# Gated products of a feed-forward transposed as float32r, by way of a transfer

## The chip, the cores and the metric

The kernel runs on one core of a Trainium2 chip. The metric is the device time of one execution in microseconds: the median of the runs. The core's engines are TensorE (PE: products and transposes; PEld: the loading of its weights), VectorE (DVE), ScalarE (ACT), GpSimd (POOL) and SyncE (SP), which issues most transfers (DMA) here. Each engine takes its instructions in order and waits at semaphores for the others.

## The reference, cut to what matters

Two layers, each with two feed-forwards around a token mixer, on 256 tokens of width 1024. So there are four feed-forwards, with an inner width of 2816:

```python
def swiglu(x, w_gate, w_up, w_down):
    return (jax.nn.silu(x @ w_gate) * (x @ w_up)) @ w_down
...
    f = swiglu(rms_norm(h, ffn1_pre_g[layer]), ffn1_w_gate[layer], ffn1_w_up[layer], ffn1_w_down[layer])
    h = h + 0.5 * rms_norm(f, ffn1_post_g[layer])
```

The change touches the product silu(x @ w_gate) * (x @ w_up), which must be turned round (channels to partitions) before it is multiplied with w_down. All inputs and outputs are float32.

## The kernel before, in words

**Precision.** TensorE multiplies in float32r, a narrower form of float32. To keep float32's precision, every operand is split in two float32r parts, hi (rounded) and lo (the rest), and every product is three: hi by hi, lo by hi, hi by lo (`mm3`, lines 179 to 183, giving L181, L182 and L183). A weight block is loaded into a float32 tile raw (five buffers), split by ScalarE (whi, L171) and VectorE (wlo, L175) into one of nine pairs of buffers, and then used by both token halves.

**Tiles and slots.** The 256 tokens are two halves, t = 0 and 1, of 128. A feed-forward (`ffn_items`, line 482) is a list of items, each a block of weights: for each of five chunks of 512 inner columns four items for the gate and four for the up product (two rows of 128 of the 1024 inputs in each), then four items for the last chunk of 256 columns, gate and up side by side in one bank (`pair_items`), then 22 items for the down product (`row_items`, one row block of w_down each). A slot (`slot`, line 365) is one item for one half: six float32r products of 512 columns. `run` (line 374) gives out the slots: half 0 goes some items ahead of half 1, soon four, and then they take turns.

**A chunk.** When the gate's sum of a half is done, ScalarE makes sil, the silu of it (L496). When the up product's sum is done, VectorE makes prod from sum and sil (L507, `post_up`). TensorE then transposes prod in blocks of 128x128 against a float32 identity into a bank tr (L515, `hidden_T`), and ScalarE and VectorE make from tr the parts hhi (L519) and hlo (L520), the operands of the down product. In `mm<-whi,xhi` the second name is the operand that sits in the array; in `tr<-ident,prod` prod sits in it and the identity streams through.

**Order.** TensorE's order is written out by the program (`tc.manual_schedule`); on the other engines a scheduler orders instructions. `defer(n, fn)` (line 81) puts a piece of work into a list, and `tick` (line 84), called at the end of each slot, runs it when its count has gone below zero: n = 2 runs two slots after the slot in which it was put there. In the kernel before, `post_up` collects both halves' prod in `made`, and when half 1 is done it defers the transposes of both by HT = 2 slots: eight transposes in a row, four in the last chunk. prod has two buffers in its pool.

**Queues.** SP issues the weight loads, the gain vectors and the small gate weights, each in its place in SP's order; a load waits on SP until the subtraction (L175) that last read its raw buffer is done. All of these go through one queue, whose transfers are spread over 16 DMA engines. `prepare_next` (line 346) decides by a pace that the program keeps by itself when the next item's load and split are put in the order.

Of the kernel before, what the change touches and what calls it, by code (L numbers as in the profile page):

```python
# [9 lines left out]
F32 = mybir.dt.float32  # L10
F32R = mybir.dt.float32r
# [5 lines left out]
P = 128  # L17
# [10 lines left out]
EPS = 1e-6  # L28
RAW = 5
WB = 9  # L30
HT = 2
LAG = 7
MID = 4
NEG = -1e30
# [10 lines left out]
def trunk_kernel(ctx: ExitStack, tc: tile.TileContext, A: dict, out: bass.AP):  # L45
    nc = tc.nc
# [3 lines left out]
    cpool = ctx.enter_context(tc.tile_pool(name="const", bufs=1))  # L50
    wpool = ctx.enter_context(tc.tile_pool(name="w", bufs=1))
    hpool = ctx.enter_context(tc.tile_pool(name="h", bufs=1))
    spool = ctx.enter_context(tc.tile_pool(name="small", bufs=4))
# [4 lines left out]
    def nm(s):  # L58
        uid[0] += 1
        return f"{s}_{uid[0]}"  # L60
# [7 lines left out]
    def trbank():  # L68
        return psum.tile([P, 512], F32, tag="tr", name=nm("tr"), bufs=2)
# [11 lines left out]
    def defer(n, fn):  # L81
        pend.append([n, fn])
# [26 lines left out]

        q.dma_start(h[t][:, a * P:b * P], A["x"][0, t * P:(t + 1) * P, a * P:b * P])  # L110

    grow0 = cpool.tile([16, P], F32, name="grow0")
    nc.scalar.dma_start(grow0, A["ffn1_pre_g"].rearrange("l (k p) -> (l k) p", p=P))
    ident = cpool.tile([P, P], F32, name="ident")
    make_identity(nc, ident)
    mhalf = cpool.tile([P, 1], F32, name="mhalf")
    nc.gpsimd.memset(mhalf, -0.5)
    warm = cpool.tile([P, 1], F32, name="warm")
# [208 lines left out]
    def gain_bcast(src):  # L327
        gb = hpool.tile([P, D], F32, tag="gb", name=nm("gb"), bufs=1)
        nc.sync.dma_start(gb, src.partition_broadcast(P))
        return gb  # L330
# [58 lines left out]
    def proj_items(w, c0, nn, get_x, post, nk=8):  # L389

        kper = min(1024 // nn, 4)
        acc = {}

        for k0 in range(0, nk, kper):
            kn = min(kper, nk - k0)

            def fetch(k0=k0, kn=kn, pieces=1):
                return load_raw(w[k0 * P:(k0 + kn) * P, c0:c0 + nn].rearrange("(k p) n -> p k n", p=P), P, kn * nn, pieces)

            def prep(fetch=fetch, kn=kn):  # L400
                return split(fetch(), P, kn * nn)

            def work(t, u, k0=k0, kn=kn, i=len(items)):
                if i < OPEN:
                    if k0 + kn == nk:
                        post(t, first_acc[t][:, :nn])
                    return
                if k0 == 0:
                    acc[t] = mmbank()
                ps = acc[t][:, :nn]  # L410
                for j in range(kn):
                    k = k0 + j
                    mm3(ps, *get_x(t, k), u.hi[:, j * nn:(j + 1) * nn], u.lo[:, j * nn:(j + 1) * nn], k == 0, k == nk - 1)
                if k0 + kn == nk:
                    post(t, acc[t][:, :nn])
            if len(items) < OPEN:
                first_loads.append(fetch)
            items.append((prep, work))

    def pair_items(wa, wb, c0, nn, get_x, post):  # L420

        acc = {}

        for k0 in range(0, 8, 2):
            def prep(k0=k0):
                raw = new_raw()
                v = raw.rearrange("p (k s n) -> p k s n", k=2, s=2)
                for s, w in enumerate((wa, wb)):
                    nc.sync.dma_start(v[:, :, s, :], w[k0 * P:(k0 + 2) * P, c0:c0 + nn].rearrange("(k p) n -> p k n", p=P))
                return split(raw, P, 1024)  # L430

            def work(t, u, k0=k0):
                if k0 == 0:
                    acc[t] = mmbank()
                for j in range(2):
                    k = k0 + j
                    mm3(acc[t], *get_x(t, k), u.hi[:, j * 512:(j + 1) * 512], u.lo[:, j * 512:(j + 1) * 512], k == 0, k == 7)
                if k0 == 6:
                    post(t, acc[t][:, :nn], acc[t][:, nn:2 * nn])
            items.append((prep, work))  # L440

    def row_items(w, widths, get_x, post, rows=2, rows0=2, late=False):

        acc = {}
        kept = [[], []]
        nk = len(widths)
        r0 = 0
        for k, kp in enumerate(widths):  # L450
            def prep(kp=kp, r0=r0, k=k):
                return split(load_raw(w[r0:r0 + kp, :], kp, D), kp, D, pin=late and k > 3)

            def work(t, u, k=k):
                if k == 0:
                    acc[t] = [mmbank(), mmbank()]
                m = rows if t == 1 else rows0
                if k >= nk - m:
                    kept[t].append((k, u))
                    if k < nk - 1:  # L460
                        return
                    todo = [(kk, uu, n) for n in range(2) for (kk, uu) in kept[t]]
                else:
                    todo = [(k, u, n) for n in range(2)]
                for (kk, uu, n) in todo:
                    mm3(acc[t][n], *get_x(t, kk), uu.hi[:, n * 512:(n + 1) * 512], uu.lo[:, n * 512:(n + 1) * 512],
                        kk == 0, kk == nk - 1)
                if k == nk - 1:
                    post(t, acc[t])
            items.append((prep, work))  # L470
            r0 += kp

    def ahead(i, fn):

        prep, work = items[i]

        def both():
            fn()
            return prep()
        items[i] = (both, work)  # L480

    def ffn_items(pool_of, wg, wu, wd, post_g, next_dests, last=False, normed=False):
        hid = {}
        sil = {}
        box = {}

        def hid_tiles(t):
            if t not in hid:
                hid[t] = (pool_of().tile([P, 22, P], F32R, tag=f"hhi{t}", name=nm("hhi"), bufs=1),
                          pool_of().tile([P, 22, P], F32R, tag=f"hlo{t}", name=nm("hlo"), bufs=1))  # L490
            return hid[t]

        def post_gate(c0, nn):
            def f(t, ps):
                s = pool_of().tile([P, 512], F32, tag="sil", name=nm("sil"), bufs=2)
                nc.scalar.activation(s[:, :nn], ps, AF.Silu, scale=rs[t][:, 0:1])  # L496
                sil[t] = s
            return f

        def post_up(c0, nn):  # L500
            made = []

            def f(t, ps):
                hh, hl = hid_tiles(t)
                s = sil[t][:, :nn]
                pr = pool_of().tile([P, 512], F32, tag="prod", name=nm("prod"), bufs=2)
                nc.vector.scalar_tensor_tensor(pr[:, :nn], ps, rs[t][:, 0:1], s, ALU.mult, ALU.mult)  # L507
                made.append((pr, hh, hl))
                if t == 1:
                    defer(HT, lambda: [hidden_T(*m) for m in made])  # L510

            def hidden_T(pr, hh, hl):
                tp = trbank()
                for j in range(nn // P):
                    nc.tensor.transpose(tp[:, j * P:(j + 1) * P], pr[:, j * P:(j + 1) * P], ident)  # L515
                k0 = c0 // P
                hv = hh[:, k0:k0 + nn // P, :].rearrange("p a b -> p (a b)")
                lv = hl[:, k0:k0 + nn // P, :].rearrange("p a b -> p (a b)")
                nc.scalar.activation(hv, tp[:, :nn], AF.Copy)  # L519
                nc.vector.tensor_tensor(lv, tp[:, :nn], hv.bitcast(F32), ALU.subtract)  # L520
            return f

        i0 = len(items)
        for i in range(5):
            proj_items(wg, i * 512, 512, main_x, post_gate(i * 512, 512))
            proj_items(wu, i * 512, 512, main_x, post_up(i * 512, 512))

        last_up = post_up(2560, 256)

        def post_both(t, pg, pu):  # L530
            post_gate(2560, 256)(t, pg)
            last_up(t, pu)

        pair_items(wg, wu, 2560, 256, main_x, post_both)

        def load_gb():
            box["gb"] = gain_bcast(post_g)

        ahead(i0 + 24, load_gb)

        def post_down(t, accs):
            enter(t, next_dests(t), accs, box["gb"], True, last, normed)

        row_items(wd, [P] * 22, lambda t, k: (hid[t][0][:, k, :], hid[t][1][:, k, :]), post_down, 4 if last else 2)
        return i0
# [803 lines left out]
```

## Time and profile before

| | |
|---|---|
| median of 3 runs | 990.96 us (990.84 to 990.96) |
| the profiled execution, first to last instruction (span) | 989.2 us |
| TensorE busy | 981.0 us, 99% of the span |
| weight loads of TensorE busy | 817.2 us, 83% |
| VectorE busy | 616.4 us, 62% |
| ScalarE busy | 528.0 us, 53% |
| queue 1 (weight loads) | 177.42 MB, 58.1% of 16 DMA engines' span |
| L515, the transposes of prod | 176 |
| L507, prod | 48 (40 of 128x512, 8 of 128x256) |

A row of the groups reads: line, engine, operation, written tile <- read tiles, shape, count, then the time in which the group was busy (us), the mean of one (ns), and the engine's idle time ahead of them. A row of the timeline reads: start (us), duration, engine, line, operation, tiles, shape, count, and in brackets the idle time before it and what ended it. TensorE's instructions overlap: the next starts while the last columns of the one before are still on their way, so the distance of starts, not the duration, tells what one costs. SPq is SP's issue of a transfer, not its flight. A row of the windows gives, for a stretch of time, its length, then busy time and instructions of each engine, then TensorE's granted clock, the DMA engines' share and GB/s.

### The profile page before, as it was taken

The numbers are of one execution on the slowest core, as the hardware profiler recorded it, in microseconds if no ns is written. First come the engines' busy times: TensorE is split into PE (matmuls) and PEld (weight loads), VectorE is DVE, ScalarE is ACT, GpSimd is POOL, SyncE is SP. The second block draws the span as 40 slices with busy tenths as digits, with TensorE's granted clock in tenths as the row PEclk, the third lists the DMA queues.
The fourth block names the chain that finished last, engine by engine and source line by source line (L and its number), as shares of the span: only waits on it lengthen the run. The fifth ranks groups of instructions, "written<-read, shape, count | busy, mean of one in ns | idle before, by whom it ended". The sixth has DMA issues, their size and how long they took to land.

```text
span 989.2 us, 12913 instructions
## 1 busy us (share of the span) xinstructions
PE 981.0 (99%) x4775; PEld 817.2 (83%) x4775; DVE 616.4 (62%) x790; ACT 528.0 (53%) x753; POOL 47.1 (5%) x92
## 2 busy tenths in 40 slices
PE   9999999999999999999999999999999999999997
PEld 6888888898978888888898888888888788888886
DVE  6756554678997555554686655554488876555542
ACT  7545443568986544443564444444366755444431
POOL 2400000100003000000100000000020000000000
PEclk9999999999999999999999999999999999999999
DMA  8967556465346766656567666655552467665531
GB/s 293 312 187 206 191 190 191 151 200 161 119 126 196 215 188 186 191 182 192 133 203 239 178 185 190 192 173 190 190 172 65 126 197 212 190 191 191 180 120 42
DMA packets 92645, 178.89 MB, mean 181 GB/s; under 512 B 11966, under 2 KB 30822, under 8 KB 92582
## 3 DMA queue, kind: packets, MB, share of 16 engines
q1 hardware_dynamic: 91142, 177.42, 58.1%
q8 instruction: 37, 0.61, 0.3%
q10 hardware_dynamic: 608, 0.53, 0.2%
q0 software_dynamic: 832, 0.12, 0.1%
q14 instruction: 26, 0.21, 0.1%
HBM read 176.95 MB, written 1.05 MB: 180 GB/s over the span
## 4 chain that ended last, share of the span: by engine, by line
PE 97%; issue 1%; DVE 1%; DMA 0%; ACT 0%; POOL 0%; POOLq 0%; ACTq 0%; DVEq 0%
PE mm L181 29%; PE mm L183 28%; PE mm L182 28%; PE tr L515 2%; PE gt L751 2%; PE gt L1053 1%; PE mm L188 1%; PE mm L1185 1%; PE mm L189 1%; PE mm L190 1%; PE mm L1088 1%; PE tr L1074 1%; PE gt L212 1%; DMA h<-in_x_dram 0%; PE tr L949 0%
## 5 line engine op out<-in xcount | busy, mean ns | idle before, releaser
L175 DVE TENSOR_TENSOR wlo<-raw,whi 128x1024 fp32r<-128x1024 f32 (+5 forms) x329 | 395.6, 1207 | 268.0 <-ACT whi L171 266.9
L171 ACT ACTIVATE whi<-raw 128x1024 fp32r<-128x1024 f32 (+5 forms) x329 | 341.9, 1046 | 333.0 <-PE mm L183 260.8
L181 PE MATMUL mm<-whi,xhi 128*128 128x512 f32 (+1 forms) x768 | 301.0, 392 | 0.0
L183 PE MATMUL mm<-whi,xlo 128*128 128x512 f32 (+1 forms) x768 | 298.2, 388 | 0.3 <-DVE xlo L226 0.3
L182 PE MATMUL mm<-wlo,xhi 128*128 128x512 f32 (+1 forms) x768 | 297.8, 388 | 0.0
L183 PEld LDWEIGHTS mm<-whi,xlo 128*128 128x128 f32 x768 | 144.2, 188 | 30.6 <-DVE xlo L226 0.7
L181 PEld LDWEIGHTS mm<-whi,xhi 128*128 128x128 f32 x768 | 144.3, 188 | 29.4 <-issue 1.3
L182 PEld LDWEIGHTS mm<-wlo,xhi 128*128 128x128 f32 x768 | 144.3, 188 | 28.4 <-DVE wlo L175 0.3
L181 PE MATMUL mm<-whi,hhi 128*128 128x512 f32 x352 | 138.0, 392 | 0.0
L183 PE MATMUL mm<-whi,hlo 128*128 128x512 f32 x352 | 137.1, 389 | 0.0
L182 PE MATMUL mm<-wlo,hhi 128*128 128x512 f32 x352 | 137.0, 389 | 0.0
L183 PEld LDWEIGHTS mm<-whi,hlo 128*128 128x128 f32 x352 | 66.1, 188 | 13.8
L181 PEld LDWEIGHTS mm<-whi,hhi 128*128 128x128 f32 x352 | 66.1, 188 | 13.4
L182 PEld LDWEIGHTS mm<-wlo,hhi 128*128 128x128 f32 x352 | 66.1, 188 | 13.3
L507 DVE SCALAR_TENSOR_TENSOR prod<-mm,rstd,sil 128x512 f32<-128x512 f32 (+1 forms) x48 | 33.9, 706 | 42.0 <-PE mm L183 34.9
L496 ACT ACTIVATE sil<-mm,rstd 128x512 f32<-128x512 f32 (+1 forms) x48 | 31.2, 652 | 40.5 <-PE mm L183 40.5
L196 POOL TENSOR_SCALAR nv<-ss 128x1 f32<-128x1 f32 x22 | 9.6, 436 | 719.7 <-ACT junk L203 719.7
L270 DVE TENSOR_TENSOR t<-mm,gb 128x512 f32<-128x512 f32 x24 | 16.2, 689 | 24.7 <-ACT junk L203 24.6
L203 ACT ACTIVATE junk<-mm 128x512 bf16<-128x512 f32 x24 | 14.3, 595 | 31.8 <-PE mm L183 31.6
L520 DVE TENSOR_TENSOR hlo<-tr,hhi 128x512 fp32r<-128x512 f32 (+1 forms) x48 | 28.7, 639 | 0.0
L181 PE MATMUL mm<-whi,zhi 128*128 128x340 f32 (+2 forms) x80 | 28.2, 353 | 0.0
L183 PE MATMUL mm<-whi,zlo 128*128 128x340 f32 (+2 forms) x80 | 27.9, 348 | 0.0
(195 smaller groups left out, 888.4 us busy)
## 6 DMA issues: line engine op xcount, KB each, us to landing
raw<-in_ffn_w_down_dram SPq DMA_DIRECT2D x88, 512.0 KB
raw<-in_ffn_w_up_dram SPq DMA_DIRECT2D x80, 512.0 KB
raw<-in_ffn_w_gate_dram SPq DMA_DIRECT2D x78, 512.0 KB
raw<-in_rg_w_in_dram SPq DMA_DIRECT2D x10, 504.0 KB
raw<-in_rg_w_out_dram SPq DMA_DIRECT2D x10, 504.0 KB
raw<-in_ffn_w_gate_dram SPq DMA_DIRECT2D x19, 256.0 KB
raw<-in_ffn_w_up_dram SPq DMA_DIRECT2D x16, 256.0 KB
raw<-in_rg_w_in_dram SPq DMA_DIRECT2D x8, 512.0 KB
```

What stands on the lines that cost most here:

```text
L171: up = nc.scalar.activation(hi[:parts, c:c + m], rawv[:, c:c + m], AF.Copy)
L175: nc.vector.tensor_tensor(lo[:parts, c:c + m], rawv[:, c:c + m], hi[:parts, c:c + m].bitcast(F32), ALU.subtract)
L181: nc.tensor.matmul(ps, xh, wh, start=first, stop=False)
L182: nc.tensor.matmul(ps, xh, wl, start=False, stop=False)
L183: nc.tensor.matmul(ps, xl, wh, start=False, stop=last)
L203: nc.scalar.activation(junk[:, :src.shape[1]], src, AF.Square, scale=f, accum_out=acc)
L270: nc.vector.tensor_tensor(t1[n], pf[n], gb[:, n * 512:(n + 1) * 512], ALU.mult)
L496: nc.scalar.activation(s[:, :nn], ps, AF.Silu, scale=rs[t][:, 0:1])
L507: nc.vector.scalar_tensor_tensor(pr[:, :nn], ps, rs[t][:, 0:1], s, ALU.mult, ALU.mult)
L515: nc.tensor.transpose(tp[:, j * P:(j + 1) * P], pr[:, j * P:(j + 1) * P], ident)
L520: nc.vector.tensor_tensor(lv, tp[:, :nn], hv.bitcast(F32), ALU.subtract)
L751: nc.tensor.matmul(ps[j][:w, g * S:(g + 1) * S], wv[rows, o:o + w], xc[rows, k, :], start=start, stop=stop, skip_group_check=True)
```

## The change

Each half's prod is now handled by itself. Behind prod, SP issues a transfer that copies it, bit for bit (`bitcast(F32)`), into a second tile, prr, which the program declares float32r. prr takes turns with prod in the same two buffers (tag "prod"). The transposes read prr and a float32r copy of the identity, identr, and write tr as float32r. HT is 4: each half's transposes stand four slots behind the slot that finished its sum, in groups of four (two in the last chunk), where before both halves' stood together two slots behind half 1. The first gain rows, grow0, move into a shared tile. What ScalarE and VectorE do with tr is unchanged.

```diff
-HT = 2
+HT = 4
...
-    grow0 = cpool.tile([16, P], F32, name="grow0")
+    grow0 = spool.tile([P, 512], F32, tag="junk", name="grow0", bufs=1)[:16, :P]
...
+    identr = cpool.tile([P, P], F32R, name="identr")
+    nc.vector.tensor_copy(identr, ident)
...
         def post_up(c0, nn):
-            made = []
-
             def f(t, ps):
                 hh, hl = hid_tiles(t)
                 s = sil[t][:, :nn]
                 pr = pool_of().tile([P, 512], F32, tag="prod", name=nm("prod"), bufs=2)
                 nc.vector.scalar_tensor_tensor(pr[:, :nn], ps, rs[t][:, 0:1], s, ALU.mult, ALU.mult)
-                made.append((pr, hh, hl))
-                if t == 1:
-                    defer(HT, lambda: [hidden_T(*m) for m in made])
-
-            def hidden_T(pr, hh, hl):
+                prr = pool_of().tile([P, 512], F32R, tag="prod", name=nm("prr"), bufs=2)
+                nc.sync.dma_start(prr[:, :nn].bitcast(F32), pr[:, :nn])
+                defer(HT, lambda: hidden_T(prr, hh, hl))
+
+            def hidden_T(prr, hh, hl):
                 tp = trbank()
                 for j in range(nn // P):
-                    nc.tensor.transpose(tp[:, j * P:(j + 1) * P], pr[:, j * P:(j + 1) * P], ident)
+                    nc.tensor.transpose(tp[:, j * P:(j + 1) * P].bitcast(F32R), prr[:, j * P:(j + 1) * P], identr)
```

## The prediction

> **What bounds the kernel now.** I read the profile's page first: the busy times, then the chain that ended last.
>
> ```profile
> span 989.2 us, 12913 instructions
> PE 981.0 (99%) x4775; PEld 817.2 (83%) x4775; DVE 616.4 (62%) x790; ACT 528.0 (53%) x753; POOL 47.1 (5%) x92
> PE 97%; issue 1%; DVE 1%; DMA 0%; ACT 0%; POOL 0%; POOLq 0%; ACTq 0%; DVEq 0%
> PE mm L181 29%; PE mm L183 28%; PE mm L182 28%; PE tr L515 2%; PE gt L751 2%; PE gt L1053 1%; PE mm L188 1%; PE mm L1185 1%; PE mm L189 1%; PE mm L190 1%; PE mm L1088 1%; PE tr L1074 1%; PE gt L212 1%; DMA h<-in_x_dram 0%; PE tr L949 0%
> ```
>
> TensorE is busy for 99% of the span, and 97% of the chain is its own work. So only two things can move the end: TensorE work that becomes shorter or longer, and TensorE standing still. Every microsecond of either counts whole. The transposes that the change touches (L515) are 2% of the chain, some 19 us; that is all there is to win.
>
> **What a transpose costs, and what it may cost.** The groups of TensorE instructions by shape give the count; the timeline gives the pace.
>
> ```profile
> L515 PE MATMUL tr<-ident,prod 128*128 128x128 f32 x176 | 23.1, 272 | 0.0
> ...
> L515 PEld LDWEIGHTS tr<-ident,prod 128*128 128x128 f32 x176 | 20.7, 140 | 3.1
> ...
> L188 PEld LDWEIGHTS mm<-xhi,whi 128*126 128x126 f32 x80 | 14.9, 186 | 0.2
> ```
> ```profile
> 36.86 1.03 PE L515 MATMUL tr<-ident,prod 128*128 128x128 f32 x8
> ...
> 139.85 0.60 PE L515 MATMUL tr<-ident,prod 128*128 128x128 f32 x4
> ...
> 239.80 0.28 PE L188 MATMUL mm<-xhi,whi 128*126 128x256 f32 x1
> ...
> 240.38 0.28 PE L190 MATMUL mm<-xhi,wlo 128*126 128x256 f32 x1
> ...
> 274.83 0.39 PE L181 MATMUL mm<-whi,y 126*128 126x512 f32 x1
> ...
> 278.91 0.39 PE L181 MATMUL mm<-whi,y 126*128 126x512 f32 x1
> ```
>
> One transpose lasts 272 ns from end to end, but they overlap: eight take 1.03 us, so they start (1030-272)/7 = 108 ns apart; four take 0.60 us, again 109. The 176 occupy 176 x 0.109 = 19.2 us. From the first quoted float32r product of 256 columns to the last are five starts in 0.58 us, 0.116 us each; from the first of 512 columns to the last 18 starts in 4.08 us, 0.227 us each. So 256 more columns cost 0.111 us, 0.43 ns a column, with next to nothing fixed. The float32 transpose, with 128 columns at 109 ns, pays 0.85 ns a column, twice that. The trace has no float32r operation of 128 columns and no float32r transpose. The line through the two sizes gives about 60 ns; I take 62, so each saves 47 ns and all of them 176 x 0.047 = **8.3 us**. The bounds: no gain (109 ns), and a loss if so narrow a float32r operation falls back to something dearer (third rival). I take 62 because it is the nearest float32r row carried on.
>
> The weight loads speak for it too. They are hidden only if 128 new columns load faster than every 62 ns. The transpose's load is 140 ns long, the ordinary product's of 126 columns 186 ns; a load that runs ahead needs less than its whole length, but how much less no row says. The Trainium skill, TensorE: Matmul & The Clock Gate, section "LDWEIGHTS (loading the stationary operand)", has a rule against the change: a load takes its column count over 1.2, in ns, whatever the rows. By that estimate 128 columns are 107 ns and the gain would be 0.4 us; here the transposes' loads are 46 ns shorter than the products' with about the same columns, which one rule for both doesn't give.
>
> **What is added.** Each prod now goes through a transfer on SP's queue (48 of them, 128x512 or 128x256), and each half is transposed by itself four slots after its own sum is done, not both halves two slots after the later one. A slot is six products of 0.227 us, 1.36 us, so the budget from the end of a sum to its transposes is 5.46 us. VectorE's prod itself, ScalarE's hhi and VectorE's hlo are issued as often as before; prod and prr take turns in the two buffers that prod had, so prod always gets one and prr the other. The identr copy and the gain rows in another tile run while the first loads of h are awaited: nothing. In the built program each prr transfer stands on SP just behind the load that the VectorE subtraction ahead of prod sets free, so SP doesn't hold it up; behind it wait later weight loads, which have five raw buffers (five times two slots, 13.6 us) of lead.
>
> How long such a transfer takes, no row shows. Two bounds. From below, the end of the kernel, where h goes out alone:
>
> ```profile
> 985.69 1.14 ACTq L286 DMA_DIRECT2D out_dram<-h  x2
> ...
> 987.00:988.10 1.10, 0.00 (x0) 0.00 (x0) 0.00 (x0) 0.00 (x0) 0.00 (x0) 1.00 0.68 227
> 988.10:989.10 1.00, 0.00 (x0) 0.00 (x0) 0.00 (x0) 0.00 (x0) 0.00 (x0) 0.51 0.00 0
> ```
>
> The second of these two pieces of 128 KB starts to be issued about 986.3 (half of the 1.14 us later than the first) and all has moved by 988.1: less than 2 us. From above, a weight load, alone and in a crowd (windows of the DMA, last columns share and GB/s; then SP's issues and ScalarE's waits for them):
>
> ```profile
> 130.62 0.33 SPq L162 DMA_DIRECT2D raw<-in_ffn_w_down_dram  x1
> ...
> 130.60:131.60 1.00, 1.00 (x6) 0.84 (x5) 1.00 (x2) 0.00 (x0) 0.00 (x0) 1.00 0.24 49
> 131.60:132.60 1.00, 1.00 (x7) 0.81 (x6) 0.19 (x1) 0.67 (x1) 0.00 (x0) 1.00 0.91 213
> 132.60:133.60 1.00, 1.00 (x6) 0.84 (x5) 0.57 (x1) 0.39 (x1) 0.00 (x0) 1.00 0.67 266
> 133.60:134.20 0.60, 0.60 (x5) 0.48 (x4) 0.60 (x1) 0.00 (x0) 0.00 (x0) 1.00 0.12 48
> 134.20:134.80 0.60, 0.60 (x4) 0.52 (x3) 0.05 (x1) 0.15 (x1) 0.00 (x0) 1.00 0.05 20
> ```
> ```profile
> 29.42 0.37 SPq L159 DMA_DIRECT2D raw<-in_ffn_w_gate_dram  x1
> ...
> 33.06 1.06 ACT L171 ACTIVATE whi<-raw 128x1024 fp32r<-128x1024 f32 x1 [0.48 <-DMA raw<-in_ffn_w_up_dram]
> 34.78 1.07 ACT L171 ACTIVATE whi<-raw 128x1024 fp32r<-128x1024 f32 x1 [0.65 <-DMA raw<-in_ffn_w_gate_dram]
> ```
>
> The lone load, issued at 130.62, has moved nearly all its bytes by 133.6 and dribbles on to about 134.8: 3.0 to 4.2 us, the last microsecond at a share of 0.05 to 0.12, about one engine of sixteen. The crowded one, issued at 29.42, is used at 34.78: 5.3 us, and the one ahead of it landed some 1.7 us earlier, so loads of one queue land one after another. A prr transfer issued behind a load therefore lands after it, by another 0.3 to 0.7 us for its own 128 or 256 KB. The Trainium skill, DMA: Bandwidth & Descriptors, section "Queues, rings and completion order", agrees with these rows: an engine takes descriptors in ring order, and the semaphore's write lands after all its earlier writes.
>
> **Where the budget holds and where not.** In the regular chunks the later half is the tight one: as in the rows of chunk five below, prod ends 0.8 us after its sum (at 126.3), and the load ahead was issued 1.1 us before that end (at 125.2), so the load lands 2 to 3.2 us after it and prr by 0.7 more, 3.9 at the latest. The transposes want it 5.46-0.8 = 4.7 us after. Held. The one place where it fails is the last chunk of each feed-forward (256 columns, gate and up in one pair), because its first half follows the second half of chunk five by one slot:
>
> ```profile
> 125.22 15.19 SPq L162 DMA_DIRECT2D raw<-in_ffn_w_down_dram  x6
> 125.55 0.75 DVE L507 SCALAR_TENSOR_TENSOR prod<-mm,rstd,sil 128x512 f32<-128x512 f32 x1 [0.36 <-PE mm L183]
> 126.96 0.47 ACT L496 ACTIVATE sil<-mm,rstd 128x256 f32<-128x256 f32 x1 [0.30 <-PE mm L183]
> 128.78 0.48 DVE L507 SCALAR_TENSOR_TENSOR prod<-mm,rstd,sil 128x256 f32<-128x256 f32 x1 [0.86 <-PE tr L515]
> 129.37 1.22 DVE L175 TENSOR_TENSOR wlo<-raw,whi 128x1024 fp32r<-128x1024 f32 x1
> ```
>
> Step by step, in these times. Sum of chunk five done 125.5; its transposes in the new order 125.5+5.46 = 131.0, done 131.2; one slot later, at 132.6, the pair's transposes. The pair's prod writes the buffer that chunk five's transfer reads. That transfer is issued at 126.3, behind the load of 125.2 (the first of the six in the row) that lands at 128.2 to 129.4, so it lands at 128.9 to 130.1. Then prod 0.5, then the subtraction of L175, 1.22: it frees a load at 130.7 to 131.9, which stands on SP *ahead* of the pair's transfer. SP issues that load (0.33 us), then the pair's transfer at 131.2 to 132.3: it also needs chunk five's transposes (131.2) to have left its buffer. The load takes its 3.0 to 4.2 us from 130.7 to 131.9, and the transfer 0.3 more: 134.0 to 136.4. TensorE stands still from 132.6: **1.4 to 3.8 us**, plus about 0.2 to start again. I take 3.0, four times: **12.0 us**, because the load quoted stands at this very place and shows the slow tail. What is late next is little: ScalarE and VectorE catch up while TensorE waits.
>
> Sum, against the profiled execution: 989.2 - 8.3 + 12.0 = 992.9. The median of the runs shown, 990.96, is 1.8 above that execution's span; so 994.7.
>
> **Rivals.**
> 1. *The transfer doesn't queue* (faster). If a transfer within SBUF doesn't wait for the load ahead, chunk five's lands at 128.3, the pair's prod runs at its old time, its transfer is issued at 131.3 and lands after the 2 us of the lower bound at 133.3: 0.7 us of standing still, four times 2.8. 989.2-8.3+2.8+1.8 = 985.5. For it: TensorE has no other new wait. Against it: loads land in turn in the rows above. It decides at 2.1 us for each pair (8.3/4), that is if the transfer lands less than 3.4 us after its issue.
> 2. *The change doesn't shorten the transpose*: 109 ns as before, because the weights' load or the passage of 32 bits sets the pace. Then 989.2+12.0+1.8 = 1003.0. The rule of the Trainium skill's TensorE page above would make the first of these true.
> 3. *A narrow float32r operation is dearer.* No float32r row is narrower than 256 columns. If at 128 it takes twice the float32 transpose, 218 ns, that is 176 x 0.109 = 19.2 us more; the standing still shrinks by the longer group (four times 0.4) to about 10: 989.2+19.2+10+1.8 = 1020.
> 4. *Both effects cancel*: the same mechanism as the forecast with the short end of its waits, 1.6 us: 989.2-8.3+6.4+1.8 = 989.1, to 2.6 us: 993. All of it within 0.2%.
>
> **How the numbers follow.** Forecast (62 ns, waits of 2.6 to 4 us) 0.46, rival 4 0.16, rival 1 0.12, rival 2 0.13, rival 3 0.13. The forecast's own range is 993 to 999. The range for all reaches down through rival 1, 986, and up through rival 2 with the long waits, 1007; that leaves out rival 3 and the tails of the others. 0.2% (2 us) is about what a measurement of this kernel can tell from no change. Faster by more than that is rival 1: 0.12. Same is rival 4: 0.16. Slower is the rest: 0.72.
>
> **What would show it.** Right: the transposes of L515 start about 62 ns apart; TensorE has four idle stretches of 2 to 4 us, each ended by the transfer of prr, at the last chunk of each feed-forward, and nowhere else; SP issues a weight load less than a microsecond ahead of that transfer. Wrong: a pace of 109 ns or more; idle stretches at regular chunks too (then transfers take over 4.7 us); or none at the last chunk.

## The result, and the profile after

| | before | after |
|---|---|---|
| median | 990.96 us (990.84 to 991.16, 4 runs) | 1009.0 us (1007.8 to 1010.31, 4 runs) |
| ratio | | 1.0178, 95% interval 1.0164 to 1.0193 |
| the profiled execution, its span | 989.2 us | 1006.1 us |
| TensorE idle for prr | none | 12.5 us |
| mean granted clock of TensorE | 0.999 | 0.993 |

The change makes the kernel 18 us slower. The forecast was 994.7, with a range of 986 to 1007. First the page of the changed kernel: span, busy times, the chain by engine.

```profile
span 1006.1 us, 13047 instructions
...
PE 985.6 (98%) x4775; PEld 816.2 (81%) x4775; DVE 617.9 (61%) x791; ACT 530.7 (53%) x753; POOL 47.2 (5%) x92
...
PE 91%; DMA 5%; DVE 2%; issue 2%; ACT 0%; POOL 0%; SPq 0%; DVEq 0%; POOLq 0%; ACTq 0%
```

TensorE's share of the chain falls from 97% to 91%, and transfers take 5% where they had none. The waits of the engines (time in all, times, the longest) and the groups of L515 tell what is waited for:

```profile
PE tr L515 <- DMA prr<-prod: 12.5, 8, 3.1
...
DVE prod L507 <- DMA prr<-prod: 5.7, 3, 2.3
```
```profile
L515 PEld LDWEIGHTS tr<-identr,prr 128*128 128x128 f32 x176 | 19.5, 140 | 21.6 <-issue 13.4
L515 PE MATMUL tr<-identr,prr 128*128 128x128 f32 x176 | 21.3, 240 | 12.5 <-DMA prr<-prod 12.5
```

TensorE waits eight times for a transfer of prr. Four of these waits are long, 2.73, 3.14, 2.68 and 2.58 us, one at the last chunk of each feed-forward. Here is the first, in the timeline of the changed kernel (lines are two further on than before, so `mm3` is L183 to L185):

```profile
125.37 0.75 DVE L507 SCALAR_TENSOR_TENSOR prod<-mm,rstd,sil 128x512 f32<-128x512 f32 x1 [0.35 <-PE mm L185]
...
126.15 0.47 SPq L509 DMA_DIRECT2D prr<-prod  x1
...
129.49 0.48 DVE L507 SCALAR_TENSOR_TENSOR prod<-mm,rstd,sil 128x256 f32<-128x256 f32 x1 [1.76 <-DMA prr<-prod]
...
129.89 1.22 DVE L177 TENSOR_TENSOR wlo<-raw,whi 128x1024 fp32r<-128x1024 f32 x1
...
130.61 0.46 PE L515 MATMUL tr<-identr,prr 128*128 128x128 f32 x4
...
131.13 0.33 SPq L164 DMA_DIRECT2D raw<-in_ffn_w_down_dram  x1
...
131.56 0.47 SPq L509 DMA_DIRECT2D prr<-prod  x1
...
135.24 0.34 PE L515 MATMUL tr<-identr,prr 128*128 128x128 f32 x2 [2.73 <-DMA prr<-prod]
...
135.41 0.46 PE L183 MATMUL mm<-whi,xhi 128*128 128x512 f32 x1
...
136.96 0.63 PE L185 MATMUL mm<-whi,xlo 128*128 128x512 f32 x1
...
137.38 0.63 PE L183 MATMUL mm<-whi,hhi 128*128 128x512 f32 x1
```

Read down: chunk five's transfer is issued at 126.15; the pair's prod waits for it until 129.49; the pair's transfer is issued at 131.56, 0.1 us behind a weight load, and TensorE gets its tile at 135.2, 3.7 us later. TensorE had been ready at 132.5. Then comes what the forecast did not have: the products at 136.96 and 137.38 are 0.63 us long and 0.42 apart, not 0.39 and 0.227. The windows of the same stretch (TensorE busy and its records first, then the other engines, then granted clock, DMA share, GB/s) say why:

```profile
128.00:132.50 4.50, 4.50 (x23) 3.39 (x21) 2.17 (x3) 2.61 (x3) 0.00 (x0) 1.00 0.59 180
132.50:135.20 2.70, 0.01 (x1) 0.00 (x0) 1.28 (x2) 0.00 (x0) 0.00 (x0) 1.00 0.92 253
...
136.30:139.60 3.30, 3.30 (x10) 2.52 (x9) 0.99 (x2) 1.06 (x1) 0.00 (x0) 0.50 0.11 38
139.70:143.00 3.30, 3.30 (x16) 2.71 (x15) 0.87 (x3) 1.42 (x2) 0.00 (x0) 1.00 0.49 158
```

After the stop the granted clock is 0.50 for a while, with 10 records in 3.3 us where the next 3.3 us have 16. In the record of the clock this stretch lasts 3.413 us, 136.249 to 139.662; there are two more of the same length, at 440.035 and 938.381, behind the second and the fourth stop. The kernel before has none until its last products have ended. In 3.413 us eight products start 0.427 apart instead of 0.227: 1.6 us lost each, 4.8 in all.

So the two profiled executions differ by 1006.1 - 989.2 = 16.9 us. Set against each other product by product, the two timelines give these parts, each to some 0.3 us. The transposes save 3.1 us: a group of four takes 0.364 us of TensorE's time, where half of a group of eight took 0.439, 40 x 0.075, and the eight pairs of the last chunk 0.1 in all. The four stops at the last chunks cost 12.1: each moves all later products back by 2.8 to 3.4 us beside the half clock; 11.1 of this is idle time. The half clock costs 4.8 (the expectations below, written from a coarser reading, split the two as 12.7 and 4.6). The remaining 3.0 lie in the first three chunks of the second and the first two of the fourth feed-forward, where four more groups of transposes find TensorE waiting for prr, 0.26 to 0.43 us each, and others start slowly because the loading of their weights waits for it. -3.1 + 12.1 + 4.8 + 3.0 = 16.8.

### The profile page after: what moved, and what is told of

Its sections match the earlier page's. It is cut to its first block, busy times and chain, and to the rows that moved or that the text cites. A ratio compares the mean times of both kernels' runs of the same rounds, so it can differ in the third digit from the quotient of the medians.

```text
span 1006.1 us, 13047 instructions
## 1 busy us (share of the span) xinstructions
PE 985.6 (98%) x4775; PEld 816.2 (81%) x4775; DVE 617.9 (61%) x791; ACT 530.7 (53%) x753; POOL 47.2 (5%) x92
## 4 chain that ended last, share of the span: by engine, by line
PE 91%; DMA 5%; DVE 2%; issue 2%; ACT 0%; POOL 0%; SPq 0%; DVEq 0%; POOLq 0%; ACTq 0%
PE mm L183 27%; PE mm L185 26%; PE mm L184 26%; DMA prr<-prod 4%; PE gt L751 1%; PE tr L515 1%; PE gt L1053 1%; PE mm L190 1%; PE mm L1185 1%; PE mm L192 1%; PE mm L191 1%; DVE wlo L177 1%; PE mm L1088 1%; DVE prod L507 1%; PE tr L1074 1%
## 5 line engine op out<-in xcount | busy, mean ns | idle before, releaser
L183 PE MATMUL mm<-whi,xhi 128*128 128x512 f32 (+1 forms) x768 | 303.1, 395 | 0.0
L185 PE MATMUL mm<-whi,xlo 128*128 128x512 f32 (+1 forms) x768 | 299.4, 390 | 0.3 <-DVE xlo L228 0.3
L185 PEld LDWEIGHTS mm<-whi,xlo 128*128 128x128 f32 x768 | 144.7, 188 | 30.7 <-DVE xlo L228 0.7
L183 PEld LDWEIGHTS mm<-whi,xhi 128*128 128x128 f32 x768 | 144.6, 188 | 28.9 <-issue 1.3
L183 PE MATMUL mm<-whi,hhi 128*128 128x512 f32 x352 | 139.3, 396 | 0.0
L185 PE MATMUL mm<-whi,hlo 128*128 128x512 f32 x352 | 138.1, 392 | 0.0
L185 PEld LDWEIGHTS mm<-whi,hlo 128*128 128x128 f32 x352 | 66.8, 190 | 14.1
L183 PEld LDWEIGHTS mm<-whi,hhi 128*128 128x128 f32 x352 | 66.9, 190 | 13.7
L519 ACT ACTIVATE hhi<-tr 128x512 fp32r<-128x512 f32 (+1 forms) x48 | 26.6, 554 | 27.7 <-PE tr L515 27.6
L520 DVE TENSOR_TENSOR hlo<-tr,hhi 128x512 fp32r<-128x512 f32 (+1 forms) x48 | 30.9, 644 | 12.9 <-ACT hhi L519 12.7
L515 PEld LDWEIGHTS tr<-identr,prr 128*128 128x128 f32 x176 | 19.5, 140 | 21.6 <-issue 13.4
L515 PE MATMUL tr<-identr,prr 128*128 128x128 f32 x176 | 21.3, 240 | 12.5 <-DMA prr<-prod 12.5
```

The lines of the kernel that those rows point to most:

```text
L183: nc.tensor.matmul(ps, xh, wh, start=first, stop=False)
L185: nc.tensor.matmul(ps, xl, wh, start=False, stop=last)
L515: nc.tensor.transpose(tp[:, j * P:(j + 1) * P].bitcast(F32R), prr[:, j * P:(j + 1) * P], identr)
```

## The experiments

The theory behind the first ones: the change is slow by the stops at the last chunk and by the half clock that follows them. The rival: the transfers disturb the kernel all over. Ratios are to the kernel before. Edits are against the changed kernel, if nothing else is said.

**last8: the last chunk transposed later.**

```diff
-        def post_up(c0, nn):
+        def post_up(c0, nn, ht=HT):
...
-                defer(HT, lambda: hidden_T(prr, hh, hl))
+                defer(ht, lambda: hidden_T(prr, hh, hl))
...
-        last_up = post_up(2560, 256)
+        last_up = post_up(2560, 256, 8)
```

> The changed kernel, but the last chunk of 256 columns defers its transposes by eight slots instead of four; nothing else differs. My theory: the 18 us are four stops of TensorE ahead of the last chunk's transposes (3.1, 3.5, 3.1 and 3.0 us, 12.7 together), three half-clock stretches behind them (1.6, 1.45 and 1.55, 4.6 together), 2 to 4 us of small stops at other chunks, less 3.3 us that the shorter transposes give. Eight slots are 5.46 us more than four, above every stop, so stops and half-clock go: 1009.0 - 12.7 - 4.6 = 991.7, range 990 to 993. Rival (the transfers disturb loads and transposes everywhere, and the last chunk is only where it shows): no more than the half comes back, 1000 or above.

Measured: 990.32 us (989.23 to 991.25), ratio 0.9992 to before, interval 0.9983 to 1.0001. 18.7 us come back by one number at four places. TensorE waits for prr nowhere, and the granted clock stays up. The rival, 1000 or above, is out: all of the loss hangs on the last chunk's deadline, but for the small stops, which were nearly gone in this run too.

**last5: later by one slot only.** The same parameter as in last8, with 5.

```diff
-        last_up = post_up(2560, 256)
+        last_up = post_up(2560, 256, 5)
```

> The changed kernel, but the last chunk defers its transposes by five slots instead of four: one slot, 1.365 us, later. My theory, in which a stop of about 3 us is also followed by half clock and a shorter one is not: each stop shrinks to 1.6 to 2.1 us, no half-clock stretch is left, 1009.0 - 4 x 1.365 - 4.6 = 998.9, range 997 to 1001. Rival A (half clock follows any stop of a microsecond or more): 1009.0 - 5.5 = 1003.5. Rival B (the half clock has nothing to do with the stops): likewise 1003.5, with the stretches at the places where they were.

Measured: 996.69 us (995.43 to 998.38), ratio 1.0056 (1.0041 to 1.0071). The four stops are 0.78, 1.43, 0.78 and 1.62 us, and no half clock follows any of them. Of the 12.3 us that came back against the changed kernel, the later deadline explains 4 x 1.365 = 5.5; the half clock 4.8; the rest, 2.0, was not traced; small stops and the spread of the landings would account for it. Rivals A and B, 1003.5, are both out: the half clock goes with the stops, not with the place, and two stops of 1.4 and 1.6 us didn't bring it.

**f32tr: the transfer without float32r.**

```diff
-                prr = pool_of().tile([P, 512], F32R, tag="prod", name=nm("prr"), bufs=2)
-                nc.sync.dma_start(prr[:, :nn].bitcast(F32), pr[:, :nn])
+                prr = pool_of().tile([P, 512], F32, tag="prod", name=nm("prr"), bufs=2)
+                nc.sync.dma_start(prr[:, :nn], pr[:, :nn])
...
-                    nc.tensor.transpose(tp[:, j * P:(j + 1) * P].bitcast(F32R), prr[:, j * P:(j + 1) * P], identr)
+                    nc.tensor.transpose(tp[:, j * P:(j + 1) * P], prr[:, j * P:(j + 1) * P], ident)
```

> The changed kernel with its transfers, its order and its stops, but prr is declared float32 and transposed against the float32 identity, so that the transposes are as dear as before. My theory: float32r saves about 19 ns in each of 176 transposes, 3.3 us, so this is slower than the changed kernel by that, 1012.3, range 1010.5 to 1014. Rival (each saves the 47 ns that I forecast, and the missing 5 us are stops elsewhere): 1009.0 + 8.3 = 1017.3.

Measured: 1010.82 us (1007.67 to 1014.4), ratio 1.0198 (1.0171 to 1.0225). The spread of the stops from run to run is as large as the difference sought, so the time alone decides only against 1017. The timelines are sharper. A regular group in f32tr, then one in the changed kernel:

```profile
121.55 0.60 PE L515 MATMUL tr<-ident,prr 128*128 128x128 f32 x4
121.91 0.47 PE L183 MATMUL mm<-whi,xhi 128*128 128x512 f32 x1
```
```profile
120.71 0.46 PE L515 MATMUL tr<-identr,prr 128*128 128x128 f32 x4
121.00 0.47 PE L183 MATMUL mm<-whi,xhi 128*128 128x512 f32 x1
```

From the group's start to the next product 0.36 us and 0.29: 0.07 us for four transposes, 18 ns each. That is the gain, and not 47.

**order: the new order alone.** The kernel before with each half transposed by itself, four slots behind its sum; no transfer, no float32r.

```diff
-HT = 2
+HT = 4
...
-                made.append((pr, hh, hl))
-                if t == 1:
-                    defer(HT, lambda: [hidden_T(*m) for m in made])
+                defer(HT, lambda: hidden_T(pr, hh, hl))
```

> The kernel before with the change's order alone: each half's prod is transposed by itself, four slots behind its sum, in groups of four, as float32 and straight from prod; no transfer and no float32r. My theory: the order costs nothing but the seams of twice as many groups, no stop at the last chunk because prod is there 4 us ahead: 991, range 990 to 992.5. Rival (the small stops at the first chunks and some of the 18 us come from the order, for instance from banks that are held in another turn): 993 to 996.

Measured: 991.91 us (991.74 to 992.46), ratio 1.0008 (0.9998 to 1.0017). The order costs about a microsecond (1.0 between the profiled executions, 1.7 at most by the interval); it stops nothing. The transposes' 3.1 us above are what is left with it.

So the place is settled. The next four ask what the stop consists of, whether the half clock comes from standing still, and what sets the pace of a transpose.

**filler: TensorE kept at work during the stop.**

```diff
                 tp = trbank()
+                if nn == 256:
+                    for _ in range(12):
+                        nc.tensor.matmul(tp, <ones, 128x128 bfloat16>, <ones, 128x512 bfloat16>, start=True, stop=True)
                 for j in range(nn // P):
```

> The changed kernel, but ahead of the last chunk's transposes of each half TensorE does twelve bfloat16 products of 128x512 that nothing needs, into the bank that the transposes then overwrite: at 0.227 us each, as the float32r products here, 2.7 us of work (96 more products in all). For half 0 they fall into the stop; for half 1 the trace shows no stop, so there they cost their full 2.7 us, four times. My theory (half clock follows because TensorE stands still for about 3 us; the stop itself is the transfer's and stays as long): half clock gone, 1009.0 - 4.6 + 4 x 2.7 = 1015.2, with no stretch of half clock. Rival (half clock comes from something else at that place, for instance from the transfers or the mix of products there): the stretches stay, 1009.0 + 10.9 = 1019.9.

Measured: 1011.51 us (1010.89 to 1012.82), ratio 1.0209 (1.0192 to 1.0226): less than either theory gave. The windows of its first last chunk:

```profile
132.00:134.90 2.90, 2.90 (x16) 1.34 (x14) 1.61 (x2) 0.23 (x1) 0.00 (x0) 1.00 0.81 278
135.00:138.00 3.00, 3.00 (x16) 2.46 (x15) 0.69 (x2) 1.45 (x2) 0.00 (x0) 1.00 0.22 87
```

The clock stays at 1.00, here and at the other three, although the transposes start hardly sooner than in the changed kernel (134.6 instead of 135.2). The half clock comes from TensorE standing still. In the trace the fillers of half 1 cost 2.6 us at each place, as expected; the four places of half 0 lost some 5 us less than in the changed kernel, where 4.6 was expected; the small stops at the first chunks happened to be 1.7 us shorter in this run. The rival's 1019.9 is out.

**poolq: GpSimd's queue for the transfers.**

```diff
-                nc.sync.dma_start(prr[:, :nn].bitcast(F32), pr[:, :nn])
+                nc.gpsimd.dma_start(prr[:, :nn].bitcast(F32), pr[:, :nn])
```

> The changed kernel, but GpSimd's queue issues the prr transfers instead of SP's; buffers and order of TensorE as they are. My theory (of the roughly 3 us of each stop, a part is the weight loads that stand ahead of the transfers in SP's queue, a part is the shared buffers): chunk five's transfer lands some 2.5 us after its issue instead of 3 to 4, the last chunk's is then issued when chunk five's transposes have left the buffer and lands 2 to 2.5 us later, 1 us behind its time; half clock gone: 1009.0 - 4.6 - 4 x 2 = 996.4, range 992 to 1000. Rival A (the queue doesn't matter, only the buffers): stops of about 3 us stay, 1009. Rival B (GpSimd issues so slowly that its transfers land later than SP's): stops at the regular chunks too, over 1012.

Measured: 1014.25 us (1014.02 to 1014.55), ratio 1.0233 (1.0218 to 1.0248). My theory missed here: the transfers stand behind no weight load any more, and the stops at the last chunks are as long as before. The timeline of the first one, and the issues of the transfers with their median time to landing:

```profile
133.28 0.55 POOL L509 DMA_DIRECT2D prr<-prod  x1 [9.37 <-DVE prod L507]
...
136.18 0.48 DVE L507 SCALAR_TENSOR_TENSOR prod<-mm,rstd,sil 128x256 f32<-128x256 f32 x1 [1.58 <-DMA prr<-prod]
...
137.48 0.46 PE L515 MATMUL tr<-identr,prr 128*128 128x128 f32 x4
...
138.23 0.55 POOL L509 DMA_DIRECT2D prr<-prod  x1 [4.40 <-PE tr L515]
...
142.09 0.34 PE L515 MATMUL tr<-identr,prr 128*128 128x128 f32 x2 [2.72 <-DMA prr<-prod]
```
```profile
prr<-prod POOLq DMA_DIRECT2D x40, 256.0 KB, 3.0
prr<-prod POOLq DMA_DIRECT2D x8, 128.0 KB, 2.6
```

The pair's transfer is issued at 138.23, after 4.40 us of waiting, as soon as the four transposes of 137.48 have left the buffer that prr shares with them; with issue and flight TensorE has its tile 3.9 us later. So the shared buffers, and the flight of a transfer with no load ahead of it in its queue, are enough for the stop. Most of the extra 5 us of this kernel is one more stop, 4.4 us, at the first chunk, where GpSimd had its own transfers to issue first.

**ownbuf: a buffer of its own for the last chunk's prod.** The order of the transposes and the queue stay as in the changed kernel.

```diff
-                pr = pool_of().tile([P, 512], F32, tag="prod", name=nm("prod"), bufs=2)
+                pr = (pool_of().tile([P, 512], F32, tag="prod", name=nm("prod"), bufs=2) if nn == 512 else
+                      spool.tile([P, 512], F32, tag="junk", name=nm("prod"), bufs=1))
```

> The changed kernel, but the last chunk's prod lies in a tile of its own (the shared tile junk, unused at that time), so that it doesn't wait for chunk five's transfer, and prr gets the buffer that chunk five's prod had, so that its transfer doesn't wait for chunk five's transposes. The built program also puts that transfer one weight load further ahead in SP's order. Transposes stay four slots behind. My theory (the stop is the chain of these two shared buffers): the transfer is issued as soon as chunk five's has landed, at 129 to 130 in the times of the first feed-forward, and lands by 132 to 133.5, where 132.6 is wanted; stops of 0 to 1 us, no half clock: 1009.0 - 12.7 - 4.6 + 2 = 993.7, range 991.5 to 997. Rival (the transfer's own flight through SP's queue is too long whenever it starts): stops of 2 us and more stay, 1000 or above.

Measured: 991.07 us (989.45 to 993.73), ratio 1.0 (0.9991 to 1.0009). Its timeline at the first last chunk, and its one wait for prr:

```profile
126.40 0.47 SPq L510 DMA_DIRECT2D prr<-prod  x1
...
126.76 1.23 DVE L177 TENSOR_TENSOR wlo<-raw,whi 128x1024 fp32r<-128x1024 f32 x1 [0.39 <-ACT whi L173]
...
127.91 0.48 DVE L508 SCALAR_TENSOR_TENSOR prod<-mm,rstd,sil 128x256 f32<-128x256 f32 x1
...
128.02 0.33 SPq L164 DMA_DIRECT2D raw<-in_ffn_w_down_dram  x1
...
129.29 0.47 SPq L510 DMA_DIRECT2D prr<-prod  x1
...
129.43 1.23 DVE L177 TENSOR_TENSOR wlo<-raw,whi 128x1024 fp32r<-128x1024 f32 x1 [1.05 <-ACT whi L173]
...
132.61 0.29 PE L516 MATMUL tr<-identr,prr 128*128 128x128 f32 x2
```
```profile
PE tr L516 <- DMA prr<-prod: 0.6, 3, 0.2
```

prod no longer waits, the transfer is issued at 129.29 instead of 131.56, behind a weight load as ever, and its flight of at most 3.3 us ends before the deadline. But this run changes two things. In the changed kernel two loads stand on SP between the two transfers, here one, and the load at 131.13 waited there for the subtraction that ended at 131.11, as late as the transposes that left the buffer at 131.07. With that load still ahead the transfer could not go before about 131.1 here, behind the subtraction that ends at 130.66, and with the same flight would land at 134.4, some 1.8 us too late (an estimate from these rows). So the shared buffers are enough to make the stop (poolq), and taking them away together with the load ahead ends it; what SP's order would cost by itself was not tried. Which of the two buffer waits (prod's for chunk five's transfer, prr's for chunk five's transposes) would be enough by itself was not tried.

**shapes: what sets the pace of a float32r transpose.** Against the kernel before:

```diff
                 for j in range(nn // P):
                     nc.tensor.transpose(tp[:, j * P:(j + 1) * P].bitcast(F32R), pr[:, j * P:(j + 1) * P], identr)
+                for j in range(nn // P):
+                    if c0 == 512:
+                        nc.tensor.transpose(tp[:64, j * P:(j + 1) * P].bitcast(F32R), pr[:, j * P:j * P + 64], identr)
+                    elif c0 == 1024:
+                        nc.tensor.transpose(tp[:, j * P:j * P + 64].bitcast(F32R), pr[:64, j * P:(j + 1) * P], identr[:64, :64])
+                    elif c0 == 1536:
+                        nc.tensor.transpose(tp[:, j * P:(j + 1) * P].bitcast(F32R), pr[:, j * P:(j + 1) * P], identr)
```

> A measurement of transposes, not of the change: VectorE writes prod straight into a float32r tile (so the parts lo are lost: prod is rounded), no transfer, both halves' transposes together two slots behind as in the kernel before. Behind the four plain transposes of each half come, in chunk two, four with only 64 columns loaded (128 streamed), in chunk three four with 64 rows and so only 64 columns streamed (128 loaded), in chunk four four plain ones again; in chunks one and five none. If the weights' load sets the pace of a float32r transpose, chunk two's extra ones cost half of chunk four's, 40 to 45 ns instead of 80 to 90, and chunk three's the full 80 to 90. If the streamed columns set it, as I had forecast, the reverse. If it is a fixed cost of each instruction, all three cost the same. A plain group of eight should take 0.65 to 0.75 us, 80 to 90 ns each; 0.50 (62 ns) would show that the transfer, not the transpose, makes them slow in the changed kernel.

Its time, 996.64 us, holds the extra transposes and says nothing by itself. Three of its groups in TensorE's timeline: chunk two, chunk three, and chunk four (all ordinary transposes).

```profile
60.27 0.46 PE L517 MATMUL tr<-identr,prod 128*128 128x128 f32 x4
60.56 0.41 PE L520 MATMUL tr<-identr,prod 128*64 128x128 f32 x4
60.81 0.49 PE L517 MATMUL tr<-identr,prod 128*128 128x128 f32 x4
61.14 0.41 PE L520 MATMUL tr<-identr,prod 128*64 128x128 f32 x4
61.38 0.44 PE L183 MATMUL mm<-whi,xhi 128*128 128x512 f32 x1
```
```profile
83.76 0.50 PE L522 MATMUL tr<-identr,prod 64*128 64x64 f32 x4
84.19 0.53 PE L517 MATMUL tr<-identr,prod 128*128 128x128 f32 x4
```
```profile
107.02 0.45 PE L517 MATMUL tr<-identr,prod 128*128 128x128 f32 x4
107.31 0.51 PE L524 MATMUL tr<-identr,prod 128*128 128x128 f32 x4
107.66 0.50 PE L517 MATMUL tr<-identr,prod 128*128 128x128 f32 x4
108.00 0.51 PE L524 MATMUL tr<-identr,prod 128*128 128x128 f32 x4
108.34 0.46 PE L183 MATMUL mm<-whi,xhi 128*128 128x512 f32 x1
```

Sixteen ordinary transposes start within 1.32 us up to the next product, 82 ns each: the first two steps are 58 and 65, the others 80 to 88. With only 64 columns loaded and still 128 streamed, they start 58 to 65 ns apart: four in 0.25 us. With all 128 columns loaded and only 64 streamed (chunk three), 84 to 86, beside some 0.18 us for each change between the shapes. So the weights' load sets the pace, at about 85 ns for 128 columns. What holds the halved load at 62 instead of 43 is not shown: the stream of 128 columns, for which the forecast had 62, or a fixed cost of each instruction; no run halved both. And there is no transfer here: the pace is the transpose's own.

**direct: float32r alone.** The kernel before with prod written straight as float32r.

```diff
-                pr = pool_of().tile([P, 512], F32, tag="prod", name=nm("prod"), bufs=2)
+                pr = pool_of().tile([P, 512], F32R, tag="prod", name=nm("prod"), bufs=2)
...
-                    nc.tensor.transpose(tp[:, j * P:(j + 1) * P], pr[:, j * P:(j + 1) * P], ident)
+                    nc.tensor.transpose(tp[:, j * P:(j + 1) * P].bitcast(F32R), pr[:, j * P:(j + 1) * P], identr)
```

> One part of the change alone, float32r without the transfer: the kernel before, but VectorE writes prod straight into a float32r tile (which rounds it, so the parts lo are lost) and TensorE transposes it as float32r, eight in a row, two slots behind, as before. It is what the change could bring at the most. My theory (128 columns of weights set a pace of about 85 ns, not 62): a group of eight takes 0.71 us instead of 0.88, a group of four 0.365 instead of 0.44; 20 x 0.167 + 4 x 0.076 = 3.6 us, 990.96 - 3.6 = 987.3, range 986.5 to 988.2. My forecast's term of 8.3 us, as the rival, would give 982.7.

Measured: 987.16 us (986.87 to 988.85), ratio 0.9963 (0.995 to 0.9977): 3.8 us (2.3 to 5.0 by the interval), where 3.6 was expected and the forecast's term was 8.3. That is the most that float32r can bring here; as prod is rounded, it is a measurement and no version to use.

**best6: the change with both cures.** ownbuf, and HT = 6.

```diff
-HT = 4
+HT = 6
...
-                pr = pool_of().tile([P, 512], F32, tag="prod", name=nm("prod"), bufs=2)
+                pr = (pool_of().tile([P, 512], F32, tag="prod", name=nm("prod"), bufs=2) if nn == 512 else
+                      spool.tile([P, 512], F32, tag="junk", name=nm("prod"), bufs=1))
```

> The changed kernel with the last chunk's prod in a tile of its own, and all transposes six slots behind their sums instead of four. My theory: no stops at the last chunk, no half clock, and the small stops that are left at the first chunks of the second and fourth feed-forward, 0.5 to 2 us in all in the other runs, have 2.7 us more of cover and go too; what stays is the transposes' gain, 3.1 us: 990.96 - 3.1 = 987.9, range 987 to 989.5. Rival (the transfers cost something beside the stops, or six slots hold up the down products): 990 or above.

Measured: 988.21 us (987.94 to 989.98), ratio 0.9973 (0.9963 to 0.9983). No wait of TensorE for prr is left. The change, without its stops, is worth 2.7 us, and this version beats both kernels.

## Why the prediction was right in part and wrong in size

**The bound: right.** Every microsecond of idle TensorE counted whole, and so did what its slower clock lost.

**The transposes' gain: mis-sized.** This is the first step that failed: "I take 62, so each saves 47 ns". `shapes` shows 62 ns with 128 columns streamed, but only once the load is halved. The loads "are hidden only if 128 new columns load faster than every 62 ns", as the text said, and they do not: about 85 ns. The inference from load durations (140 ns against 186) carried no price and was let stand for one. The term is 3.1 us in the changed kernel and 3.8 in `direct`, not 8.3: 5.2 us of the miss. The rule of the Trainium skill that was weighed there (TensorE: Matmul & The Clock Gate, "LDWEIGHTS (loading the stationary operand)", by which the prediction estimated 107 ns for 128 columns) named the right cause, the load by its columns, with too high a price. The same page of the Trainium skill, section "Back-to-back issue gap", states about 81 ns for a sustained stream of loads and 128-column products; the 82 ns on average measured here agree with that, and it was overlooked.

**The four stops: right in place and size, the cause in part.** Four, at the last chunk of each feed-forward, each ended by the transfer of prr, in the timeline shown with a weight load issued 0.1 us ahead of it; 12.1 us in all where 12.0 was taken. That the size came out so close is luck in part: 3.0 was a choice out of 1.4 to 3.8. Of the chain, the buffers were enough by themselves: the pair's prod waits for chunk five's transfer, the pair's transfer for chunk five's transposes. The load ahead in SP's queue, which the forecast added to the flight, was not needed for a stop of this length (poolq).

**The half clock: not foreseen.** The forecast ended the account of a stop with "about 0.2 to start again". In three of the four cases 3.4 us at half clock came behind it, 1.6 us lost each: 4.8 us of the miss. The kernel before shows no long stop of TensorE to learn this from, but its page has a row of the granted clock, and the question what a stop does to it was not asked. That the third stop, 2.68 us, brought no half clock is a matter of where it fell (last section). The Trainium skill, TensorE: Matmul & The Clock Gate, section "What's actually happening", states that the clock falls to half after an idle window of about 3.4 us, 3413 ns and free-running; the stretches of 3.413 us agree with that length, but stops well below it were enough here.

**"And nowhere else": wrong by 3.0 us.** The regular chunks were said to hold their budget, 4.7 us against 3.9 "at the latest". In the first chunk of the second feed-forward VectorE was at a subtraction when the sum was done, so prod came 0.9 us later than reckoned, and the transfer, issued behind a load, took 4.2 us:

```profile
322.73 1.23 DVE L177 TENSOR_TENSOR wlo<-raw,whi 128x1024 fp32r<-128x1024 f32 x1 [4.61 <-ACT whi L173]
...
323.87 0.74 DVE L507 SCALAR_TENSOR_TENSOR prod<-mm,rstd,sil 128x512 f32<-128x512 f32 x1
...
323.98 0.37 SPq L161 DMA_DIRECT2D raw<-in_ffn_w_up_dram  x1
...
324.64 0.47 SPq L509 DMA_DIRECT2D prr<-prod  x1
...
328.83 0.53 PE L515 MATMUL tr<-identr,prr 128*128 128x128 f32 x4 [0.43 <-DMA prr<-prod]
```

Of the reckoned 3.9, the 0.7 us for a transfer's own 256 KB was short too: the loads that the prediction quotes land 1.7 us apart for 512 KB each, 0.85 for half of it. A budget that holds by 0.8 us with an upper bound of one quoted load is not a budget that holds everywhere.

**The sum.** In the profiled execution the forecast had 992.9 for a span of 1006.1: 13.2 too low, of which 5.2 are the transposes, 4.8 the half clock, 3.0 the small stops and 0.1 the four stops. The rivals: none was the case by itself. Rival 2 (no gain at all from float32r, 1003.0) came nearest in time, for a reason that was half true. Rival 1 needed the pair's transfer to land less than 3.4 us after its issue; it took 3.7 here, up to the start of the transposes, and 3.9 even on a queue with no load ahead of it.

## What to carry to other kernels

When a copy is put between a producer and a deadline, follow its buffers before its queue: two tiles that take turns in a ring chain each copy to the end of the one before, and the tightest pair of deadlines decides. Price a stop of TensorE with the clock that follows it, and price a small TensorE instruction by the loading of its weights as well as by its stream. A deadline moved by a few slots was the cheapest cure here: it gave back all 18 us.

## What the runs showed of the hardware that was not expected

- **Half clock after short stops.** In all traces together there are thirteen stops of TensorE of 2.1 to 4.4 us (idle time before the next record). After nine of them the granted clock fell to 0.5 for 3.413 us: behind stops of 2.11, 2.43, 2.58, 2.63, 2.73, 2.93, 3.14, 3.45 or 4.39 us, while one each of 2.10, 2.68, 2.72 and 3.24 had no such stretch. Six of 0.73 to 1.62 us ahead of these transposes had none. The half clock began between 0.4 us before and 1.4 us after TensorE started again. So length alone does not decide. What does can be read from the record of the clock: in every trace, each change of the clock lies a whole number of steps of 3.4133 us behind the first one (in the changed kernel 129.706, 300.373 and 494.933 us at full clock, that is 38, 88 and 145 steps). Count TensorE's idle time in each of these steps. In the nine steps ahead of a half clock it is 2.03 to 3.17 us; in the steps of the other stops it is 1.72 at most. The third stop of the changed kernel is cut by an edge into 1.39 and 1.30 us. So two microseconds or more without work inside one such step cost the clock of the next one; no run shows a step between 1.81 and 2.03.
- **The pace of transposes.** float32: 109 ns apart; float32r: about 85 in a running group with 128 columns loaded, about 62 with 64.
- **Change of shape.** Between transposes of 128 and of 64 rows the next start came 0.18 us later instead of 0.085 us (in `shapes`, chunk three).
- **Copies within SBUF.** From GpSimd's queue 128 KB land 2.6 us and 256 KB 3.0 us after the issue (medians): twice the bytes add only 0.4 us.
